# The last four blocks' gate and up in the 7-product form, and w_down of six blocks by token halves

## The chip, the cores and the metric

The kernel runs on one core of one Trainium2 chip, as one program. The metric is the device time of one execution in microseconds; lower is better. The engines that matter here are TensorE (PE in the profile; its weight loads are PEld), VectorE (DVE), ScalarE (ACT) and SyncE (SP), whose queue issues the kernel's transfers.

## The reference

One decoder layer on x of 1024 tokens by 1024 features, all in float32:

```python
x = _layer_norm(ALPHA * x + 0.5 * _swiglu(x, ffn1_w_gate[i], ffn1_w_up[i], ffn1_w_down[i]), ...)
mix = _token_mixer(x, w_in[i], ...)          # four GDN heads, four GLA heads, w_out
x = _layer_norm(ALPHA * x + mix, ...)
x = _layer_norm(ALPHA * x + 0.5 * _swiglu(x, ffn2_w_gate[i], ffn2_w_up[i], ffn2_w_down[i]), ...)

def _swiglu(x, w_gate, w_up, w_down):
    return (jax.nn.silu(x @ w_gate) * (x @ w_up)) @ w_down
```

The hidden width of each feed-forward layer (FFN) is 2816, that is 22 blocks of 128. The change is in the second FFN and the layer norm that ends the layer.

## The kernel before

**Numbers.** Every large product is made of three matmuls: each operand is split into a high part (a cast on ScalarE) and a low part (a subtraction on VectorE), and high by high, low by high and high by low are added up in one bank of PSUM. `split` (lines 139 to 141) is that pair of instructions, so the profile shows nearly all splits as L140 and L141. A weight half, a hidden half or an x tile is 128 partitions by 512 columns, 256 KB. It is loaded by SP into a staging tile (tag `wr`, seven of them) and split into tiles that TensorE reads.

**Tiles.** x stands transposed, by token half (512 tokens) and feature block: `xh[half][k]`, `xl[half][k]`, k from 0 to 7. The layer's output rows are eight tiles `acc[c]` of 128 tokens by 1024, four to a token half; w_down adds to them by columns 0 to 511 and 512 to 1023.

**Plain form.** `hidden` (line 358) makes one block of 128 hidden features: per token half 8 x 3 matmuls for gate and as many for up (`proj`, lines 212 to 215), each 512 columns wide. `down` (line 218) adds w_down of several blocks to one output half tile: 3 matmuls a block in a bank tagged `pd` (three of these), then one VectorE instruction (line 239) that scales the bank and adds it to `acc`.

**7-product form.** `ffn_pairs` (line 729) takes the blocks two at a time. Gate, and then up, of two blocks for both token halves is a 2 by 2 by 2 product of quarters; `project` (line 512) makes it from 7 products of 4 x 3 matmuls (lines 554 to 556) where the plain form has 8. For this `token_sums` and `last_sums` keep sums of x quarters (named P5, P6, P3 and P7; P7 is written over x tiles 10 to 13, half 1, k 0 to 3), and `weight_sums` (line 479) makes sums of weight quarters on VectorE. `PRODUCTS` (line 47) is the order: P1, P2, P6, P5, P7, P4, P3. P1 and P2 read x of the first token half, P4 reads x tiles 14 to 17. The four results are complete after P2 (first half, first block), P7 (second half, second block), P4 (second half, first block) and P3 (first half, second block). The function given as `hidden` takes each result; `put` (line 568) writes it to device memory some turns later.

**Down steps.** w_down of the pairs' blocks is interleaved with the products. Two groups of four blocks use a 7-product form as well (`down_four`, lines 688 to 693, 28 steps of 6 matmuls each). Blocks 16 and 17 are done plainly (`down_two`, 16 steps of 6 matmuls through `down`). `STEPS` (line 53) says how many steps go with each pair; within a pair they are spread over its 14 products. Operands are made up to five (`DEEP`) ahead of their use.

**Order of the second FFN.** Blocks 0 to 7 are done plainly, partly beside the mixer. Then `ffn_pairs(2, range(8, 18))` does blocks 8 to 17 in five pairs (line 1288). Then `last_blocks` (line 402) does blocks 18 to 21 plainly: it loads x tiles 10 to 13 again (`restore`), and for each token half makes four hidden blocks (gate and up weights are loaded and split anew for each half) and calls `last_downs` (line 412), which loads the four blocks' w_down (again for each half) and goes through the four token tiles: the column halves of one tile, its statistics (`out_stats`), and beside the next tile its rows (`out_rows`: normalise, scale, store). The last tile's second column half is cut in two of 256, so that the end is short.

**Who sets the order.** A framework puts the written program into one stream for each engine. It works from the written order, but an instruction whose inputs are there may be placed ahead of earlier written ones that still wait; semaphores follow from the tiles that are read and written. Each engine then goes through its stream in order, SP included.

## Time and profile before

| | |
|---|---|
| median of 3 runs | 2027.14 us (2026.97, 2027.14, 2030.98) |
| the profiled execution | 2030.06 us, of which the span from first to last instruction is 2028.3 us |
| granted TensorE clock, mean | 0.998 |
| moved by DMA | 313.63 MB, mean 155 GB/s |

The span is what the views of the profile cover, with time counted from its start; the other 1.8 us lie around it. The views used are the page (busy time of each engine, the chain of waits that ended last), the windows view (busy time in chosen stretches), the groups (instructions by line, tiles and shape, with count, busy time and the mean of one), the timeline (start, duration, engine, line, what is written and read, and in brackets idle time before it and what ended it), the waits and the DMA issues. A matmul's duration overlaps the next one's, so the spacing of starts is what it costs.

### The profile page before, as it was taken

What the parts mean: (1) busy time and instruction counts of PE and PEld (TensorE: products, weight loads), DVE (VectorE), ACT (ScalarE), POOL (GpSimd) and SP (SyncE); (2) the same over time, 40 slices, a digit from 0 to 9 for tenths busy, and PEclk for the clock granted to TensorE, in tenths of its full rate; (3) what the DMA queues carried; (4) which work ended last, traced back from release to release, by engine and by line L of the source; (5) the groups of instructions that cost most, each with busy time, mean ns of one, the idle gap of its engine ahead of it and who ended that gap; (6) DMA issues with size and microseconds to landing.
All of it is one profiled execution on the core that took longest, in us unless ns stands there. A gap on an engine that the chain in (4) does not pass through costs nothing.

```text
span 2028.3 us, 28810 instructions
## 1 busy us (share of the span) xinstructions
PE 1995.8 (98%) x9956; PEld 1632.1 (80%) x9956; DVE 1435.8 (71%) x3043; ACT 875.2 (43%) x1739; POOL 50.3 (2%) x87
## 2 busy tenths in 40 slices
PE   8999999999999999999999999999999999999998
PEld 7888888888888777788788777788788888888887
DVE  7677776545677787756887687657956657888565
ACT  5333433222554445445566545444433433334332
POOL 0000000000000000000000000000000000000000
PEclk9999999999999999999999999999999999999999
DMA  8755645655553444445364433333443336466431
GB/s 268 264 173 166 202 142 167 205 195 192 171 191 128 136 149 142 135 134 169 127 197 130 132 106 122 104 105 109 135 142 119 114 117 200 156 212 204 146 121 61
DMA packets 170930, 313.63 MB, mean 155 GB/s; under 512 B 19360, under 2 KB 19872, under 8 KB 170784
## 3 DMA queue, kind: packets, MB, share of 16 engines
q1 hardware_dynamic: 170784, 311.80, 48.1%
q8 instruction: 78, 1.28, 0.3%
q14 instruction: 68, 0.56, 0.1%
HBM read 244.61 MB, written 67.11 MB: 154 GB/s over the span
## 4 chain that ended last, share of the span: by engine, by line
PE 84%; DVE 8%; DMA 3%; ACT 3%; issue 2%; POOL 1%; SPq 0%; DVEq 0%; ACTq 0%; POOLq 0%
PE pa L212 11%; PE pa L213 11%; PE pa L215 11%; PE pa L554 6%; PE pa L555 6%; PE pa L556 6%; PE pd L234 5%; PE pd L236 5%; PE pd L235 5%; PE pm L689 1%; PE pm L688 1%; PE pm L690 1%; PE pm L1211 1%; DVE acc L239 1%; PE pm L810 1%
## 5 line engine op out<-in xcount | busy, mean ns | idle before, releaser
L140 ACT CAST wh<-wr 128x512 fp32r<-128x512 f32 (+1 forms) x485 | 298.3, 620 | 645.6 <-PE pa L213 201.6
L212 PE MATMUL pa<-xh,wh 128*128 128x512 f32 x1168 | 469.9, 402 | 9.3 <-ACT xh L140 5.6
L141 DVE TENSOR_TENSOR wl<-wr,wh 128x512 fp32r<-128x512 f32 (+1 forms) x485 | 329.5, 686 | 203.6 <-ACT wh L140 199.1
L213 PE MATMUL pa<-xl,wh 128*128 128x512 f32 x1168 | 461.4, 395 | 0.1
L215 PE MATMUL pa<-xh,wl 128*128 128x512 f32 x1152 | 454.1, 394 | 0.0
L212 PEld LDWEIGHTS pa<-xh,wh 128*128 128x128 f32 x1168 | 220.9, 189 | 56.0 <-ACT xh L140 6.3
L213 PEld LDWEIGHTS pa<-xl,wh 128*128 128x128 f32 x1168 | 220.9, 189 | 42.6 <-DVE xl L141 2.1
L215 PEld LDWEIGHTS pa<-xh,wl 128*128 128x128 f32 x1152 | 217.2, 189 | 43.2
L239 DVE SCALAR_TENSOR_TENSOR acc<-pd,acc 128x512 f32<-128x512 f32 x305 | 205.3, 685 | 50.5 <-PE pd L236 48.9
L234 PE MATMUL pd<-wh,hh 128*128 128x512 f32 x352 | 141.1, 405 | 1.5 <-ACT xf L283 1.5
L235 PE MATMUL pd<-wl,hh 128*128 128x512 f32 x352 | 139.5, 397 | 1.0 <-DVE wl L141 1.0
L236 PE MATMUL pd<-wh,hl 128*128 128x512 f32 x352 | 138.9, 397 | 0.0
L554 PE MATMUL pa<-xh,wh 128*128 128x512 f32 x320 | 125.5, 392 | 0.5 <-DVE gs L530 0.5
L555 PE MATMUL pa<-xl,wh 128*128 128x512 f32 x320 | 124.6, 389 | 0.0
L556 PE MATMUL pa<-xh,wl 128*128 128x512 f32 x320 | 124.6, 389 | 0.0
L154 ACT CAST wh<-wr 128x512 fp32r<-128x512 f32 x132 | 80.0, 620 | 84.4 <-PE pa L213 63.6
L155 ACT CAST wl<-wr 128x512 fp32r<-128x512 f32 x132 | 81.0, 618 | 42.8 <-PE pd L235 39.1
L234 PEld LDWEIGHTS pd<-wh,hh 128*128 128x128 f32 x352 | 66.3, 188 | 19.6 <-ACT hh L140 4.1
L236 PEld LDWEIGHTS pd<-wh,hl 128*128 128x128 f32 x352 | 66.1, 188 | 14.9 <-DVE hl L141 2.5
L234 PE MATMUL pd<-wh,gh 128*128 128x512 f32 (+1 forms) x194 | 75.8, 393 | 1.4 <-DVE acc L239 1.2
L235 PEld LDWEIGHTS pd<-wl,hh 128*128 128x128 f32 x352 | 66.4, 189 | 12.6 <-DVE wl L141 1.4
L236 PE MATMUL pd<-wh,gl 128*128 128x512 f32 (+1 forms) x194 | 75.1, 388 | 0.0
(399 smaller groups left out, 3478.5 us busy)
## 6 DMA issues: line engine op xcount, KB each, us to landing
wr<-gu SPq DMA_DIRECT2D x263, 256.0 KB, 3.1
wr<-wd SPq DMA_DIRECT2D x172, 256.0 KB, 2.9
kept<-wl SPq DMA_DIRECT2D x132, 256.0 KB, 2.2
wr<-kept SPq DMA_DIRECT2D x132, 256.0 KB, 2.8
wr<-win SPq DMA_DIRECT2D x116, 256.0 KB, 3.1
wr<-hid SPq DMA_DIRECT2D x106, 256.0 KB, 2.9
hid<-gs SPq DMA_DIRECT2D x44, 256.0 KB, 2.6
hid<-wr SPq DMA_DIRECT2D x32, 256.0 KB, 3.3
```

The source lines that it names most:

```text
L140: self.nc.scalar.copy(hi, src)
L141: self.nc.vector.tensor_tensor(lo, src, hi.bitcast(F32), ALU.subtract)
L212: nc.tensor.matmul(ps[:], hi[:, sl], xh[k][:], start=(k == 0), stop=False)
L213: nc.tensor.matmul(ps[:], hi[:, sl], xl[k][:], start=False, stop=(lo is None and k == KB - 1))
L215: nc.tensor.matmul(ps[:], lo[:, sl], xh[k][:], start=False, stop=(k == KB - 1))
L234: nc.tensor.matmul(p, hh[:, sl], wh[:, ds], start=(i == 0), stop=False)
L235: nc.tensor.matmul(p, hh[:, sl], wl[:, ds], start=False, stop=False)
L236: nc.tensor.matmul(p, hl[:, sl], wh[:, ds], start=False, stop=(i == n - 1))
L239: nc.vector.scalar_tensor_tensor(acc, p, scale / ALPHA, acc, ALU.mult, ALU.add, accum_out=None if sums is None else sums[:, d:d + 1])
L554: nc.tensor.matmul(ps[:], op[0][:, sl], xh[:], start=new, stop=False, skip_group_check=True)
L555: nc.tensor.matmul(ps[:], op[0][:, sl], xl[:], start=False, stop=False, skip_group_check=True)
L556: nc.tensor.matmul(ps[:], op[1][:, sl], xh[:], start=False, stop=q == 3, skip_group_check=True)
```

## The change

The last four blocks also go through `ffn_pairs`, now over blocks 8 to 21 in seven pairs. The queue of down steps then holds the two groups of four only, 56 steps, spread over pairs three to seven. Nothing of w_down of blocks 16 to 21 is in the steps; `last_blocks` does it, for six blocks, plainly, by token halves.

For the last pair `last_pair` takes the results: those of the first token half are split at once into x tiles that are no longer read (06 and 07); those of the second go to device memory. `last_blocks` has no gate and up and no `restore`. It loads and splits w_down once for both token halves, and the hidden halves of the first token half that are in memory, into x tiles that have come free (`x_room`) and into tiles of its own pool; later the second token half's hidden halves. The first group of the first token half is two token tiles side by side, in which block 21 comes last in both (`ahead` is 2). Staging tiles go from seven to ten.

```diff
-BUFS = {"w": 6, "h": 3, "xf": 3, "wr": 7, ...
+BUFS = {"w": 6, "h": 3, "xf": 3, "wr": 10, ...
-STEPS = {1: (0, 14, 14, 18, 18), 2: (0, 0, 14, 14, 20)}
+STEPS = {1: (0, 14, 14, 18, 18), 2: (0, 0, 10, 10, 12, 12, 12)}
-LAST = 4
+LAST = 6
 def down(...):
-                                               accum_out=None if sums is None else sums[:, d:d + 1])
+                                               accum_out=sums[c][:, d:d + 1] if sums and c in sums else None)
 def out_stats(...):
-            self.rows = [self.ln_row(2, 0), self.ln_row(2, 1, ("hh", "hl"), BUFS["h"])]
+            self.rows = [self.ln_row(2, 0), self.ln_row(2, 1, ("g1", "b1"))]
+    def x_room(self, n):
+        return [self.wt(self.xp, [HT], f"x{e}{n // KB}{n % KB}", 1, F32R) for e in "hl"]
+
+    def last_pair(self, f):
+        def take(n, t=None):
+            if t is None:
+                return
+            if n[0] == "1":
+                hl = self.first_half[f + int(n[1]) - 1] = self.x_room(5 + int(n[1]))
+                self.split(hl[0][:], hl[1][:], t[:])
+            else:
+                self.put((f, 1, int(n[1]) - 1), t)
+        return take
+
     def last_blocks(self, fs):
         with self.phase("ep") as fx:
             self.hp = fx
-            self.scr = "xf", fx
-            for k in range(KB // 2):
-                self.restore(1, k)
-            for half in range(2):
-                hs = [now(self.hidden(2, f, (half,), fx, ("gh", "gl"), BUFS["g"])) for f in fs]
-                self.last_downs(fs, hs, half, fx)
+            free = list(range(6)) + list(range(8, 16))
+            def parts(t):
+                hl = self.x_room(free.pop(0)) if free else [self.wt(fx, [HT], "g" + e, len(fs) + 4, F32R) for e in "hl"]
+                self.split(hl[0][:], hl[1][:], t[:])
+                return hl
+            ws = [[parts(self.load(self.a["wd2"][f][:, HALVES[0]]))] for f in fs]
+            hs = [parts(self.load(self.hbm[(2, f - f % 2), 0, f % 2][:])) for f in fs[:-2]] + [self.first_half[f] for f in fs[-2:]]
+            for w, f in zip(ws, fs):
+                w.append(parts(self.load(self.a["wd2"][f][:, HALVES[1]])))
+            self.last_downs(hs, ws, 0, ([0, 1], [2], [3]))
+            hs = [parts(self.load(self.hbm[(f - f % 2, 1, f % 2) if f in fs[-2:] else ((2, f - f % 2), 1, f % 2)][:])) for f in fs]
+            self.last_downs(hs, ws, 1, ([0], [1], [2], [3]))
-    def last_downs(self, fs, hs, half, fx):
-        ws = [self.weight(self.a["wd2"][f], *((fx, "f") if 2 * n < BUFS["f"] else ())) for n, f in enumerate(fs)]
-        for c in range(4):
+    def last_downs(self, hs, ws, half, groups):
+        before = range(4)[-1:] if half else []
+        for cs in groups:
...
+            work = self.down(hs, ws, half, 0.5, cs, sums,
+                             ((0, HT), (HT, HT + HT // 2), (HT + HT // 2, D)) if last else ((0, HT), (HT, D)), len(cs))
...
 def ffn_pairs(...):
-        queue = [(idx, f, 4) for f in fours] + [(idx, f, 2) for f in range(start + 8, fs.stop, 2)]
+        queue = [(idx, f, 4) for f in fours] + [(idx, f, 2) for f in range(start + 8, fs.stop, 2) if idx == 1]
-            take = self.lone_pair(g) if g[1] not in fours else ...
+            take = self.last_pair(f) if f == NF - 2 else self.lone_pair(g) if g[1] not in fours else ...
 def run(self):
-            self.ffn_pairs(2, range(K2, NF - LAST), 0, beside=...)
+            self.ffn_pairs(2, range(K2, NF), 0, beside=...)
+            for _ in range(2):
+                self.turn += 2
+                self.put_now()
         self.last_blocks(range(NF - LAST, NF))
```

## The prediction

> **What bounds the kernel now.** I read the page first, for the engines' totals and the chain of waits.

> ```profile
> span 2028.3 us, 28810 instructions
> PE 1995.8 (98%) x9956; PEld 1632.1 (80%) x9956; DVE 1435.8 (71%) x3043; ACT 875.2 (43%) x1739; POOL 50.3 (2%) x87
> PE 84%; DVE 8%; DMA 3%; ACT 3%; issue 2%; POOL 1%; SPq 0%; DVEq 0%; ACTq 0%; POOLq 0%
> ```

> TensorE is busy 98% of the span and makes 84% of the chain. An average hides stages, so the second view is the windows view, cut where the timeline of TensorE changes from one kind of matmul to the next. The columns are window, length, then busy time (instructions) of PE, PEld, DVE, ACT and POOL, granted clock, DMA share and GB/s.

> ```profile
> 600.00:1460.00 860.00, 844.05 (x4842) 685.88 (x4841) 643.79 (x1738) 429.54 (x963) 40.37 (x61) 1.00 0.42 133
> 1598.72:1852.66 253.94, 253.94 (x1117) 208.92 (x1115) 184.85 (x294) 97.29 (x171) 0.00 (x0) 1.00 0.52 167
> 1852.66:1866.26 13.60, 13.60 (x62) 11.27 (x60) 12.54 (x22) 5.39 (x9) 0.00 (x0) 1.00 0.72 233
> 1866.26:1889.53 23.27, 22.36 (x97) 17.86 (x96) 18.07 (x30) 7.44 (x13) 0.00 (x0) 1.00 0.57 169
> 1889.53:1933.05 43.52, 43.52 (x193) 36.04 (x192) 18.84 (x28) 16.34 (x28) 0.00 (x0) 1.00 0.46 141
> 1933.05:1954.82 21.77, 21.77 (x97) 18.01 (x96) 16.63 (x38) 7.32 (x17) 1.66 (x3) 1.00 0.18 70
> 1954.82:1998.34 43.52, 43.52 (x193) 36.04 (x192) 23.29 (x39) 15.73 (x27) 0.84 (x1) 1.00 0.35 113
> 1998.34:2028.30 29.96, 22.11 (x109) 18.52 (x107) 20.99 (x48) 5.19 (x13) 2.55 (x4) 0.91 0.19 73
> ```

> In order these are: the mixer; the five block pairs in the 7-product form with the first down steps between; the rest of the second group of four; w_down of blocks 16 and 17; gate and up of the last four blocks for the first token half; their w_down; the same two for the second half, with the tail. From 1598.72 on TensorE is never idle except in the 1866.26 window and the tail, and in the stage that the change replaces VectorE and ScalarE are far from full. There the time is the number of matmuls times the spacing of two. The timeline's first column (start) gives that spacing:

> ```profile
> 1880.01 0.39 PE L234 MATMUL pd<-wh,gh 128*128 128x512 f32 x1
> 1880.24 0.39 PE L235 MATMUL pd<-wl,gh 128*128 128x512 f32 x1
> ```

> It is 0.23 us (the 0.39 is the length of one, overlapping the next); closer, 43.52 us over the 192 matmuls that the code issues there is 0.2267 us. [...]

> **Gate and up of blocks 18 to 21.** The grouped view of the last stages (line, operands, count) shows what goes:

> ```profile
> L212 PE MATMUL pa<-xh,wh 128*128 128x512 f32 x128 | 49.8, 389 | 0.0
> L213 PE MATMUL pa<-xl,wh 128*128 128x512 f32 x128 | 49.8, 389 | 0.0
> L215 PE MATMUL pa<-xh,wl 128*128 128x512 f32 x128 | 49.8, 389 | 0.0
> ```

> That is 3 x 128 = 384 matmuls. In their place come two more pairs: 2 pairs x 2 (gate, up) x 7 products x 4 chunks x 3 = 336. The difference is 48 x 0.2267 = 10.9 us off TensorE, the one engine that is full here. [...]

> **w_down.** The two groups of four keep their 336 matmuls. Blocks 16 and 17 (96) and 18 to 21 (96, then 84 of 512 and 24 of 256 columns, since the last token tile is cut) become six blocks in one form: 144, then 126 and 36. So 6 fewer of 512 and 12 more of 256 columns, whose spacing is read here, with the tail:

> ```profile
> 2020.05 0.28 PE L235 MATMUL pd<-wl,gh 128*128 128x256 f32 x1
> 2020.17 0.28 PE L236 MATMUL pd<-wh,gl 128*128 128x256 f32 x1
> 2020.95 0.41 DVE L239 SCALAR_TENSOR_TENSOR acc<-pd,acc 128x256 f32<-128x256 f32 x1
> 2024.51 0.99 SPq L334 DMA_DIRECT2D out_dram<-acc  x2
> ```

> 12 x 0.12 - 6 x 0.2267 = +0.1 us: nothing.

> **The stall that goes.** The 1866.26 window is 23.27 us for 96 matmuls, 21.77 us at the spacing, so it loses 1.5 us. Most of it is one place:

> ```profile
> 1874.57 0.39 PE L236 MATMUL pd<-wh,gl 128*128 128x512 f32 x1
> 1875.78 0.50 PE L234 MATMUL pd<-wh,gh 128*128 128x512 f32 x1 [0.82 <-DVE acc L239]
> ```

> Two-block sums hold a bank for only 6 matmuls (1.36 us), and VectorE, late with x splits and hidden splits, frees the banks late. Afterwards a sum takes 18 matmuls (4.1 us) with 0.60 us of VectorE to free it (starts below). I take -1.5 us. What is late next is the seam, below.

> **The tail.** The last matmul ends at 2020.17 + 0.28 = 2020.45, its accumulation starts at 2020.95: VectorE was still with the rows of the tile before. A token tile then has 8.2 us of matmuls rather than 5.4, so those rows are done sooner: -0.5 us. The rest is the same code.

> **More 7-product work.** The 1598.72 window holds 840 + 276 = 1116 matmuls, 253.0 us, and takes 253.94: 0.9 us lost over ten gate or up halves. Four more cost +0.4 us.

> **The seam.** The new wait is at the start of w_down for the first token half. It needs six split w_down halves, four hidden halves loaded back (blocks 16 to 19), and both blocks of the last pair, one of which leaves the last product. The x tiles that receive them come free after the last up half's second product (x00 to x05) and its P7 (x10 to x13). After that second product TensorE still has five products of 2.72 us and six steps of 1.36 us: 21.8 us of cover. What must fit in it is priced by these rows, the first two the pace of VectorE, the next three the landing (last column, us):

> ```profile
> 1861.40 0.68 DVE L693 SCALAR_TENSOR_TENSOR acc<-pd,acc 128x512 f32<-128x512 f32 x1
> 1862.00 0.68 DVE L141 TENSOR_TENSOR gl<-wr,gh 128x512 fp32r<-128x512 f32 x1
> wr<-wd SPq DMA_DIRECT2D x172, 256.0 KB, 2.9
> wr<-hid SPq DMA_DIRECT2D x106, 256.0 KB, 2.9
> hid<-gs SPq DMA_DIRECT2D x44, 256.0 KB, 2.6
> ```

> Ten loads are 2.6 MB, 11 us at the 233 GB/s of the 1852.66 window, and ten staging tiles let all be under way at once. Ten lower parts on VectorE are 6.0 us; its own work there is some 73% of 21.8, 16 us, less about 4 us because weight parts are made five operands ahead and run out before the end: 18 of 21.8. It fits, narrowly. The block from the last product (add, multiply, cast, subtract: 2.7 us) is hidden by the step behind that product, 1.36 us, and by the order of the first group, whose two tiles take that block last, 30 matmuls or 6.8 us in. The six halves for columns 512 to 1023 are due 36 matmuls, 8.2 us, after the start and cost 3.6 us of VectorE. I take +0.5 us for the whole seam, with 0 below (it cannot give time) and 7.7 above (first rival).

> What joins SP's queue: 10, then 6, then 6 loads and the four writes of the last pair's hidden halves, which wait for VectorE; only loads due later stand behind them. The second half's tokens go through memory (write 2.6 us, load 2.9) and are due 144 matmuls, 32.6 us, later. Dropped are the four x restores and 16 of 32 gate and up weight loads. All this lies beside TensorE: zero, unless VectorE fills.

> **The sum.** -10.9 + 0.1 - 1.5 - 0.5 + 0.4 + 0.5 = -11.9 us. The profiled execution spans 2028.3 us and took 2030.06; it would span 2016.4 and take 2018.2. The median of the runs, 2027.14, lies 2.9 below the profiled one; less 11.9 that is **2015.2 us**.

> **Rival 1: the seam opens.** The splits are written behind the last product. If ScalarE and VectorE keep that order, nothing starts before the last product ends: 2.7 us for its block, then seven splits at 0.60 and a first cast, 4.8 us, less the step's 1.36: 6.1 us idle. A pause also slows what follows:

> ```profile
> 1003.69 0.40 PE L236 MATMUL pd<-wh,hl 128*128 128x512 f32 x1
> 1005.88 0.80 PE L212 MATMUL pa<-xh,wh 128*128 128x512 f32 x1 [1.79 <-DVE wh L824]
> 1006.47 0.63 PE L213 MATMUL pa<-xl,wh 128*128 128x512 f32 x1
> ...
> 1008.61 0.63 PE L212 MATMUL pa<-xh,wh 128*128 128x512 f32 x1
> 1009.03 0.49 PE L234 MATMUL pd<-wh,hh 128*128 128x512 f32 x1
> ```

> After 1.8 us idle seven matmuls take from 1005.88 to 1009.03, 3.15 us, a spacing of up to 0.43 us where 7 x 0.2267 is 1.59: 1.6 us more. That makes 7.7 in all, and the time 2015.2 - 0.5 + 7.7 = 2022.4. [...] Against this rival: work written later does run earlier where its inputs are there.

> ```profile
> 1870.97 0.62 ACT L140 CAST xh<-wr 128x512 fp32r<-128x512 f32 x1 [0.92 <-DMA wr<-x2d]
> 1873.79 1.14 ACT L140 CAST gh<-wr 128x512 fp32r<-128x512 f32 x2
> ```

> The x casts of the last blocks stand ahead of hidden casts of blocks 16 and 17, which the code writes first. Chance 0.14.

> **Rival 2: slower, by the mixer.** Ten staging tiles serve the whole kernel, and a different arrival of weights gives ScalarE and VectorE another order between 600 and 1460 us, where TensorE waits on short chains.

> ```profile
> PEld pm L1083 <- ACT mi L1081: 9.5, 28, 0.4
> ```

> There 860 - 844.05 = 16 us are idle. A weight split that runs ahead of a chain's step delays it by 0.60 us. Slower by 0.2% (4.1 us, about what a measurement of this kernel can tell from no change) needs 11.9 + 4.1 = 16 us, or 27 such delays, as much idle time again: 2031.3 or more. Against it: the six pairs of split-weight tiles stay, and they, not the staging, decide when a split may run. Chance 0.07. The same shuffle could also give back a quarter of those 16 us.

> **Rival 3: the second column half is late.** If none of its six splits is done when the first group ends, 3.6 us more: 2018.8. For it: VectorE's narrow margin. Against: 8.2 us are due to it. Chance 0.07.

> **How the numbers follow.** The forecast has 0.72. Faster by over 0.2% (below 2023.0) are it, rival 3, and about a third of rival 1 after allowing for its coarse price: 0.84. Within 0.2%: the rest of rival 1, 0.08. Slower: rival 2, rounded up to 0.08 for what I have not thought of. The range reaches down to 2010 (no seam, and the quarter of 16 us gained) and up to 2023 (rival 1); it leaves out rival 2 and the ends of the others.

> **What would show it.** Right: no L212 to L215 group in the last 180 us; 1176 matmuls of L554 to L556's kind in the second FFN, not 840; from the first pair to the end of the last matmul some 410 us (before: 1598.72 to 2020.45, 421.7); TensorE unbroken between the last product and w_down; the mixer's idle time near 16 us. Wrong: a gap of microseconds at the seam with 0.43 us spacing behind it (rival 1), over 25 us idle in the mixer (rival 2), or gaps within the first token half that VectorE's splits end (rival 3).

## The result, and the profile after

| | before | after |
|---|---|---|
| median of 4 runs | 2027.88 us (2026.97 to 2030.98) | 2014.47 us (2013.18 to 2017.16) |
| ratio, 95% interval | | 0.9933 [0.9916, 0.9950] |
| profiled execution | 2030.06, span 2028.3 | 2013.18, span 2011.4 |

Faster by 13.4 us, where 11.9 were forecast; 2014.47 lies 0.7 below the predicted 2015.2, and the other 0.7 is in the kernel before, whose median is 2027.88 with a fourth run. Below, "the pairs' stretch" is the time from the first block pair of the second FFN to the end of the last matmul. It is the part of the kernel that the change rewrites.

The page of after, span, busy time and chain of waits:

```profile
span 2011.4 us, 28705 instructions
PE 1982.5 (99%) x9914; PEld 1622.3 (81%) x9914; DVE 1429.9 (71%) x3037; ACT 869.3 (43%) x1733; POOL 50.3 (3%) x87
PE 86%; DVE 8%; ACT 2%; DMA 2%; issue 1%; POOL 0%; SPq 0%; DVEq 0%; ACTq 0%; POOLq 0%
```

TensorE has 42 matmuls fewer (48 gone, 6 gained by finer cuts) and is still what bounds the kernel. The windows view of after, with the same columns as before (window, length, then busy time and instructions of PE, PEld, DVE, ACT, POOL, clock, DMA share, GB/s), shows the mixer, the pairs, the stretch just ahead of w_down, w_down of the first and of the second token half, and the tail:

```profile
600.00:1460.00 860.00, 844.82 (x4850) 686.50 (x4849) 646.77 (x1742) 430.13 (x964) 40.31 (x61) 1.00 0.42 134
1594.76:1938.83 344.07, 344.02 (x1513) 283.10 (x1511) 244.57 (x388) 135.43 (x237) 0.00 (x0) 1.00 0.47 154
1900.00:1938.83 38.83, 38.83 (x173) 31.96 (x171) 31.43 (x51) 19.17 (x33) 0.00 (x0) 1.00 0.56 173
1938.83:1971.50 32.67, 32.67 (x146) 27.07 (x145) 21.71 (x47) 9.36 (x21) 1.65 (x3) 1.00 0.26 93
1971.50:2004.50 33.00, 33.00 (x163) 27.89 (x161) 20.49 (x47) 4.57 (x12) 2.54 (x4) 1.00 0.16 65
2004.50:2011.40 6.90, 0.00 (x0) 0.00 (x0) 3.92 (x8) 0.00 (x0) 0.90 (x1) 0.88 0.20 76
```

TensorE has no gap worth naming from the first pair to the last matmul. VectorE is at 81% (31.43 of 38.83) ahead of w_down: close, not full. The mixer has 860 - 844.82 = 15.2 us idle, before 15.95: no reordering to speak of.

The pairs' stretch in one row, first before, then after:

```profile
1598.72:2020.45 421.73, 420.81 (x1860) 346.65 (x1858) 290.57 (x485) 154.70 (x276) 4.14 (x7) 1.00 0.47 150
```

```profile
1594.76:2004.50 409.74, 409.69 (x1818) 338.06 (x1816) 286.78 (x481) 149.36 (x270) 4.19 (x7) 1.00 0.43 142
```

So the 16.9 us by which the two spans differ are 12.0 in this stretch, 0.95 in the tail (7.85 to 6.90) and 4.0 ahead of the first pair, where the change edits nothing but the number of staging tiles. The last part is taken up with the experiments: some 2 us of it go with the number of staging tiles, and 1.6 are a short time at half the TensorE clock in the profile of before (clock column 0.50 from 1005.83 to 1009.24).

The seam, in the timeline of after (start, duration, engine, line, operands, in brackets idle time before it and what ended it). The last step of the pairs ends in L719, w_down begins in L235:

```profile
1938.60 0.39 PE L719 MATMUL pm<-wh,gl 128*128 128x512 f32 x1
1938.83 0.39 PE L235 MATMUL pd<-xh,xh 128*128 128x512 f32 x1
...
1931.76 2.67 ACT L141 CAST xh<-wr 128x512 fp32r<-128x512 f32 x4 [1.76 <-PE pa L585]
1939.11 0.63 ACT L141 CAST xh<-gs 128x512 fp32r<-128x512 f32 x1 [4.68 <-DVE gs L569]
...
1935.60 0.68 DVE L142 TENSOR_TENSOR xl<-wr,xh 128x512 fp32r<-128x512 f32 x1
```

The spacing stays 0.23 us across the seam. The splits of w_down and of the hidden halves into x tiles (`xh<-wr`, `xl<-wr`) are over at 1936.3, although the code writes them behind the last product; they are 14, the ten needed at the start and four of the six for the second column half. Of what the first sums need, only the block of the last product (`xh<-gs`) is split behind the seam, and ScalarE waited 4.7 us for it without harm. The last two w_down halves and the second token half's hidden halves follow it.

The tail, in the timeline of after:

```profile
2004.22 0.28 PE L237 MATMUL pd<-gh,gl 128*128 128x256 f32 x1
2004.54 0.42 DVE L240 SCALAR_TENSOR_TENSOR acc<-pd,acc 128x256 f32<-128x256 f32 x1 [1.07 <-PE pd L237]
2007.92 0.99 SPq L335 DMA_DIRECT2D out_dram<-acc  x2
```

VectorE now waits for the last matmul and follows it by 0.04 us; before it came 0.50 behind. That is half of the 0.95; the rest lies behind it, in the last rows and their store.

### The profile page after: what moved, and what is told of

It is laid out like the page before. It is cut to its first block, busy times and chain, and to the rows that moved or that the text cites. A ratio compares the mean times of both kernels' runs of the same rounds, so it can differ in the third digit from the quotient of the medians.

```text
span 2011.4 us, 28705 instructions
## 1 busy us (share of the span) xinstructions
PE 1982.5 (99%) x9914; PEld 1622.3 (81%) x9914; DVE 1429.9 (71%) x3037; ACT 869.3 (43%) x1733; POOL 50.3 (3%) x87
## 4 chain that ended last, share of the span: by engine, by line
PE 86%; DVE 8%; ACT 2%; DMA 2%; issue 1%; POOL 0%; SPq 0%; DVEq 0%; ACTq 0%; POOLq 0%
PE pa L213 9%; PE pa L214 9%; PE pa L216 9%; PE pa L583 8%; PE pa L584 7%; PE pa L585 7%; PE pd L235 6%; PE pd L237 6%; PE pd L236 6%; PE pm L718 1%; PE pm L717 1%; PE pm L719 1%; PE pm L1240 1%; DVE wl L142 1%; PE pm L839 1%
## 5 line engine op out<-in xcount | busy, mean ns | idle before, releaser
L141 ACT CAST wh<-wr 128x512 fp32r<-128x512 f32 (+1 forms) x469 | 289.5, 620 | 666.7 <-PE pa L584 204.4
L142 DVE TENSOR_TENSOR wl<-wr,wh 128x512 fp32r<-128x512 f32 (+1 forms) x469 | 318.1, 685 | 195.1 <-ACT wh L141 185.8
L213 PE MATMUL pa<-xh,wh 128*128 128x512 f32 x1040 | 419.2, 403 | 9.2 <-ACT xh L141 5.3
L214 PE MATMUL pa<-xl,wh 128*128 128x512 f32 x1040 | 411.3, 396 | 0.1
L216 PE MATMUL pa<-xh,wl 128*128 128x512 f32 x1024 | 404.3, 395 | 0.0
L213 PEld LDWEIGHTS pa<-xh,wh 128*128 128x128 f32 x1040 | 196.3, 189 | 51.2 <-ACT xh L141 6.5
L240 DVE SCALAR_TENSOR_TENSOR acc<-pd,acc 128x512 f32<-128x512 f32 x289 | 194.2, 684 | 56.7 <-PE pd L237 55.0
L214 PEld LDWEIGHTS pa<-xl,wh 128*128 128x128 f32 x1040 | 196.4, 189 | 37.6 <-DVE xl L142 2.1
L216 PEld LDWEIGHTS pa<-xh,wl 128*128 128x128 f32 x1024 | 193.2, 189 | 38.2
L583 PE MATMUL pa<-xh,wh 128*128 128x512 f32 x384 | 150.6, 392 | 0.2 <-DVE sn L568 0.2
L584 PE MATMUL pa<-xl,wh 128*128 128x512 f32 x384 | 149.5, 389 | 0.0
L585 PE MATMUL pa<-xh,wl 128*128 128x512 f32 x384 | 149.5, 389 | 0.0
L235 PE MATMUL pd<-wh,hh 128*128 128x512 f32 x352 | 140.9, 404 | 1.5 <-ACT xf L284 1.4
L236 PE MATMUL pd<-wl,hh 128*128 128x512 f32 x352 | 139.4, 397 | 1.0 <-DVE wl L142 1.0
L583 PEld LDWEIGHTS pa<-xh,wh 128*128 128x128 f32 x384 | 72.1, 188 | 18.7 <-DVE sn L568 2.2
L585 PEld LDWEIGHTS pa<-xh,wl 128*128 128x128 f32 x384 | 72.1, 188 | 15.1
L584 PEld LDWEIGHTS pa<-xl,wh 128*128 128x128 f32 x384 | 72.1, 188 | 14.6
L235 PEld LDWEIGHTS pd<-wh,hh 128*128 128x128 f32 x352 | 66.2, 188 | 19.6 <-ACT hh L141 4.2
## 6 DMA issues: line engine op xcount, KB each, us to landing
wr<-gu SPq DMA_DIRECT2D x247, 256.0 KB, 3.4
wr<-wd SPq DMA_DIRECT2D x164, 256.0 KB, 3.0
kept<-wl SPq DMA_DIRECT2D x132, 256.0 KB, 2.1
wr<-kept SPq DMA_DIRECT2D x132, 256.0 KB, 3.0
wr<-win SPq DMA_DIRECT2D x116, 256.0 KB, 3.2
wr<-hid SPq DMA_DIRECT2D x110, 256.0 KB, 3.3
hid<-gs SPq DMA_DIRECT2D x50, 256.0 KB, 2.1
hid<-wr SPq DMA_DIRECT2D x32, 256.0 KB, 3.0
```

The lines of the kernel that those rows point to most:

```text
L141: self.nc.scalar.copy(hi, src)
L142: self.nc.vector.tensor_tensor(lo, src, hi.bitcast(F32), ALU.subtract)
L213: nc.tensor.matmul(ps[:], hi[:, sl], xh[k][:], start=(k == 0), stop=False)
L214: nc.tensor.matmul(ps[:], hi[:, sl], xl[k][:], start=False, stop=(lo is None and k == KB - 1))
L216: nc.tensor.matmul(ps[:], lo[:, sl], xh[k][:], start=False, stop=(k == KB - 1))
L235: nc.tensor.matmul(p, hh[:, sl], wh[:, ds], start=(i == 0), stop=False)
```

## The experiments

Each ratio is to the kernel before, run on the same chip in the same series. It is given with its 95% interval, and differs from the quotient of the two medians by up to 0.001. "Changed kernel" is the kernel of the change.

**Ten staging tiles alone.** The kernel before, with one size changed.

```diff
-BUFS = {"w": 6, "h": 3, "xf": 3, "wr": 7, ...
+BUFS = {"w": 6, "h": 3, "xf": 3, "wr": 10, ...
```

> The kernel before with ten staging tiles instead of seven, nothing else. Two theories. Count theory: the gain is the 48 matmuls, the stall and the tail; in the stages before the pairs of the second FFN staging depth changes nothing that counts, and the 4.0 us by which the changed profile reaches the first of these pairs earlier (1594.76 against 1598.72) are the spread between executions. Then this run is the kernel before within 0.1%, a ratio of 1.000, and its mixer (600 to 1460 us) keeps some 16 us idle. Staging theory: deeper staging itself gives about 4 us ahead of the pairs. Then the ratio is 0.998 and the first pair starts 4 us earlier.

Measured: 2027.62 against 2029.74, 0.9989 [0.9980, 0.9998]. The row of the pairs' stretch:

```profile
1595.33:2017.21 421.88, 420.85 (x1860) 346.59 (x1858) 288.80 (x485) 153.82 (x276) 4.13 (x7) 1.00 0.45 148
```

421.9 us, as before. Ten tiles alone give the stretch nothing; what small gain they give (0.4 to 4 us by the interval) lies outside it. The profiles show where. All kernels but the last of this section have a pause of 2.2 us on TensorE near 1000 us, ahead of the same matmul. It ends at 1003.2 to 1004.3 in the seven profiles with ten tiles, at 1005.9 to 1006.3 in the three with seven, and at 1009.0 in the one with eight. So ten tiles gain some 2 us before that point, by these profiles, and the measured ratio lies between the two theories.

Inside the stretch the tiles only move a loss. The stage of the two-block steps, in which the prediction found its stall, takes 22.15 us here rather than 23.27:

```profile
1864.12:1886.27 22.15, 22.15 (x98) 17.87 (x96) 17.44 (x28) 7.18 (x13) 0.00 (x0) 1.00 0.57 178
```

Instead TensorE waits for VectorE in pair three, where 1.17 us lie between two starts at 1692.55.

**The changed kernel with seven staging tiles.** The same edit the other way round, `"wr": 10` to `"wr": 7` in the changed kernel.

> The changed kernel with the seven staging tiles of before. Count theory: ahead of the pairs no difference; at the seam the last three of the ten loads wait for a split, which 21.8 us of cover hide, so 2014.5 us, ratio to the kernel before 0.993 to 0.994, no gap ahead of w_down. Staging theory: 4 us more than the changed kernel, 2018.5 us, ratio 0.9955. If the ten tiles are what keeps the seam closed: a gap of 2 to 4 us between the last product and w_down, with 0.43 us spacing behind it.

Measured: 2029.24, ratio 0.9988 [0.9977, 0.9998]. Nearly the whole gain is gone, and all expectations missed the place: the seam is unbroken here too (the 6.58 us that TensorE is idle in the stretch are the 2.97 and 3.61 of two stops elsewhere). TensorE stops at the first down step of pair three, and again at that of pair five. The timeline of the first stop, PE and then SP:

```profile
1682.23 0.39 PE L585 MATMUL pa<-xh,wl 128*128 128x512 f32 x1
1685.59 0.97 PE L717 MATMUL pd<-wh,gh 128*128 128x512 f32 x3 [2.97 <-ACT wh L141]
1687.35 0.63 PE L717 MATMUL pd<-wh,gh 128*128 128x512 f32 x1
1687.78 0.63 PE L718 MATMUL pd<-wl,gh 128*128 128x512 f32 x1
...
1676.97 0.45 SPq L601 DMA_DIRECT2D hid<-wr  x1
...
1680.36 0.32 SPq L601 DMA_DIRECT2D hid<-wr  x1
1680.77 1.25 SPq L485 DMA_DIRECT2D wr<-wd  x2
```

The step waits for a cast of w_down (`wh`, L141), the cast for its load, and SP issues the step's two loads from 1680.77 on, 1.7 us before it is due (1682.46). Just ahead of them in the queue are the last two of four writes `hid<-wr`: the sums of hidden halves that `second_pair` keeps in staging tiles until they are written to memory, and that wait for VectorE. In the changed kernel the same two loads go out from 1654.19 on, 23 us before their step (1677.11) and ahead of all four writes. So with fewer tiles the framework places these loads later in SP's stream:

```profile
1654.19 2.65 SPq L485 DMA_DIRECT2D wr<-wd  x2
...
1668.90 1.04 SPq L601 DMA_DIRECT2D hid<-wr  x2
```

The second stop is longer:

```profile
1790.62 0.39 PE L585 MATMUL pa<-xh,wl 128*128 128x512 f32 x1
1794.62 0.97 PE L717 MATMUL pd<-wh,gh 128*128 128x512 f32 x3 [3.61 <-ACT wh L141]
```

Less a normal spacing each, the two stops are (3.36 - 0.23) + (4.00 - 0.23) = 6.9 us; behind the first, matmuls go at 0.43 us from 1686.92 to 1689.91, and behind the second the one at 1795.88 lasts 0.52 us, where the one before it took 0.39. Pair five, like pair three, follows a pair that makes such sums. The pairs' stretch is 420.4 us for the same 1818 matmuls, 10.7 more than with ten tiles.

**Eight staging tiles**, `"wr": 10` to `"wr": 8`.

> The changed kernel with eight staging tiles, steps as in the change. Theory of held tiles: with eight held at the first step of pairs three and five, eight tiles still leave none for the w_down loads, so stops of 2 to 4 us remain there, somewhat shorter than in E2, ratio 0.996 to 0.998. If one tile is enough to let the first load through: stops under 1 us, ratio 0.9935 to 0.995.

Measured: 2026.09, ratio 0.9974 [0.9964, 0.9984], in the range that the theory of held tiles gave. Its second stop in the timeline:

```profile
1789.56 0.40 PE L719 MATMUL pd<-wh,gl 128*128 128x512 f32 x1
1792.24 1.09 PE L717 MATMUL pd<-wh,gh 128*128 128x512 f32 x2 [2.29 <-ACT wh L141]
```

From start to start that is 2.7 us here and 1.4 at 1684.75, in the same two pairs, shorter than with seven (the one at 1684.75 below the 2 to 4 us expected), and the stretch takes 415.8. SP's queue ahead of the first stop lies between the other two: one of the two loads goes out behind two of the four writes, the other behind all four.

```profile
1675.39 1.05 SPq L601 DMA_DIRECT2D hid<-wr  x2
...
1678.11 0.43 SPq L485 DMA_DIRECT2D wr<-wd  x1
1678.63 0.88 SPq L601 DMA_DIRECT2D hid<-wr  x2
...
1681.71 0.33 SPq L485 DMA_DIRECT2D wr<-wd  x1
```

The cost falls with every tile added: 420.4, 415.8, 409.7 us with seven, eight and ten.

**Seven tiles, and the steps of before's first pairs.** In the kernel before, seven tiles cause no such stop. There the pairs three and four take 14 steps each, here 10, so that the first step comes later in the pair and its operands, made five ahead, are asked for among later weights.

```diff
-BUFS = {... "wr": 10, ...     STEPS = {..., 2: (0, 0, 10, 10, 12, 12, 12)}
+BUFS = {... "wr": 7, ...      STEPS = {..., 2: (0, 0, 14, 14, 10, 10, 8)}
```

> The changed kernel with seven staging tiles and the steps at 14, 14, 10, 10, 8 instead of 10, 10, 12, 12, 12. Run E2 stopped TensorE for 3.4 and 4.0 us at the first down step of pairs three and five, not at the seam. Theory of held tiles: with 10 steps the first step stands behind the pair's second product, so four raw gate or up tiles are loaded ahead of its w_down and stay in use, beside four that the pair before still holds for its sums: eight, one more than there are. With 14 steps it stands behind the first product, two raw tiles ahead, six in all, and the w_down loads find room: no stop over 1.5 us there, ratio 0.9935 to 0.995, the rest of the way to E2 being what ten tiles give ahead of the pairs. If seven tiles are too few for seven pairs whatever the order: stops as in E2 and a ratio of 0.998 or more.

Measured: 2024.13 (2019.43 to 2025.84), ratio 0.9968 [0.9956, 0.9980], between the expectations. The profile has no stop at 1682: the two loads go out at 1656.59 and 1665.55, ahead of the four writes (from 1672.45 on). It has 1.7 us at 1781.9 (a wait for VectorE) and 1.0 us at 1797.6 (again for a cast of w_down), around the start of pair five, which has 10 steps here; its stretch is 412.4 us. So the step schedule explains the first stop; the later ones are shorter with it, and not gone. The profiled execution was this kernel's shortest; what the others lose beyond it was not seen.

**Gate and up alone.** The changed kernel, with w_down of blocks 16 and 17 in the steps and of 18 to 21 by token halves, as before.

```diff
-STEPS = {..., 2: (0, 0, 10, 10, 12, 12, 12)}    LAST = 6
+STEPS = {..., 2: (0, 0, 14, 14, 14, 14, 16)}    LAST = 4
-        queue = ... for f in range(start + 8, fs.stop, 2) if idx == 1]
+        queue = ... for f in range(start + 8, fs.stop if idx == 1 else NF - LAST, 2)]
```

> One part of the change alone: gate and up of the last four blocks in the 7-product form, but w_down of blocks 16 and 17 stays in the down steps (72 steps: 14, 14, 14, 14, 16 with pairs three to seven), and four blocks are left for the end by token halves. Count theory: the 48 matmuls are all gone here too, so 10.9 us less, and up to 1.5 us more if the two-block steps no longer stall now that products lie between them: 2015.5 to 2017 us, ratio 0.994 to 0.995. If instead w_down of six blocks alone carries the gain: less than half of it here, 2021 us or more.

Measured: 2017.76 against 2029.74, ratio 0.9931 [0.9919, 0.9944]: as fast as the changed kernel (0.9933 and 0.9917 in two other series), as far as the timing tells. The row of the stretch, and then VectorE near the end:

```profile
1596.81:2007.68 410.87, 409.78 (x1812) 337.60 (x1810) 294.88 (x496) 150.56 (x272) 4.19 (x7) 1.00 0.42 142
```

```profile
2006.80 0.75 DVE L333 SCALAR_TENSOR_TENSOR acc<-xf,mv,b 128x512 f32<-128x512 f32 x1
...
2008.45 0.41 DVE L240 SCALAR_TENSOR_TENSOR acc<-pd,acc 128x256 f32<-128x256 f32 x1
```

In the profiles it stands 1.1 us behind the changed kernel in the stretch and 1.1 in the tail (2007.68 to the end of the span at 2015.7 is 8.0). The tail shows why: VectorE is still with the rows of the tile before (L333) when the last sums come, and starts the last one 0.8 us behind the last matmul. The 1.1 of the stretch is one stop: TensorE waits for VectorE from 1694.12 to 1695.54 in pair three, as the kernel before does with ten tiles. So the rest of the change, w_down of six blocks and the steps that this leaves, is worth some 2 us by two profiles; the timings don't resolve it.

**48 matmuls put back.** The changed kernel makes P1 of the last two pairs twice, over the same bank: 2 pairs x 2 (gate, up) x 12 matmuls more.

```diff
-            for q, (xh, xl) in enumerate(self.tokens(n)):
+            for q, (xh, xl) in list(enumerate(self.tokens(n))) * (2 if twice and n == "P1" else 1):
-                make = self.project(ops, hid, up, take)
+                make = self.project(ops, hid, up, take, idx == 2 and f >= NF - 4)
```

> The changed kernel with 48 matmuls put back: in the last two pairs the first product of each gate and up half is made twice (the second time overwrites the first with the same values), on operands that are there anyway; nothing else is added. Count theory (TensorE is full in the pairs, so 48 matmuls are 48 x 0.2267 us): 10.9 us more than the changed kernel, ratio to the kernel before 0.9987. If the gain came from the other engines' relief or from staging, the repeat would lie beside them: under half of that, ratio 0.996 or less.

**The changed kernel once more**, in the same series, as its yardstick.

> The changed kernel once more, on the chip and in the rounds of the other three, with its own profile. Ratio 0.9933 as measured before, within 0.001. The stretch from the first pair of the second FFN to the last matmul repeats to 0.5 us (409.7 us); what differs between its executions lies ahead of it, where a pause near 1003 us is or is not followed by half-rate matmuls (1.5 us).

Measured: 2024.81, ratio 0.9972 [0.9961, 0.9983], and 2013.37, ratio 0.9917 [0.9904, 0.9930]. The rows of the stretch, with the 48 and without:

```profile
1596.78:2017.32 420.54, 420.54 (x1866) 347.07 (x1864) 287.23 (x481) 149.27 (x270) 4.20 (x7) 1.00 0.42 139
```

```profile
1598.14:2007.78 409.64, 409.64 (x1818) 337.99 (x1816) 286.73 (x481) 149.37 (x270) 4.19 (x7) 1.00 0.43 142
```

48 matmuls, 10.90 us in the stretch and 11.4 in the medians: the main term of the sum, by itself. (The expectation counted its ratio from 0.9933; against the yardstick of its own series it is 0.0055, that is 11.2 us.) The second row also shows how well a stretch repeats: 409.64 here, 409.74 in the first profile of the same program, while the first pair starts at 1598.14 and 1594.76. Of the 3.4 us between these two, the last section shows the cause: in the second profile TensorE has half its clock for 6.8 us near 1003, in the first never there. Of the 4.0 us between before and after, 2.1 are there when the pause near 1000 ends (1005.88 and 1003.80), and 1.6 come right behind it, from half the clock for 3.41 us in before: 19 matmuls behind the end of the pause the two are 6.04 and 4.46 us on (1011.92 and 1008.26).

**The splits in their written order.** The changed kernel, with the casts and subtractions of `last_blocks` held where the code writes them.

```diff
-    def split(self, hi, lo, src):
-        self.nc.scalar.copy(hi, src)
-        self.nc.vector.tensor_tensor(lo, src, hi.bitcast(F32), ALU.subtract)
+    def split(self, hi, lo, src, pin=lambda i: i):
+        pin(self.nc.scalar.copy(hi, src))
+        pin(self.nc.vector.tensor_tensor(lo, src, hi.bitcast(F32), ALU.subtract))
...
-                self.split(hl[0][:], hl[1][:], t[:])
+                self.split(hl[0][:], hl[1][:], t[:], self.tc.keep_in_program_order)
```

> The changed kernel with every split that the last stage writes pinned on ScalarE and VectorE behind all that is written before it, so that the w_down and hidden splits wait for the last product of the last pair (rival 1 of the prediction, made to happen). By the prediction's working: 6.1 us idle between the last product and w_down and 1.6 us of half-rate matmuls behind it, 7.7 us in all, about 2022 us, ratio 0.997. If the seam is covered whichever way the splits stand: 2014.5 us and no gap.

Measured: 2022.91, ratio 0.9961 [0.9948, 0.9975]. The first rival, made to happen; PE and then ScalarE in the timeline:

```profile
1937.99 0.39 PE L719 MATMUL pm<-wh,gl 128*128 128x512 f32 x1
1942.81 0.50 PE L235 MATMUL pd<-xh,xh 128*128 128x512 f32 x1 [4.43 <-ACT xh L141]
...
1944.11 0.79 PE L237 MATMUL pd<-xh,xl 128*128 128x512 f32 x1 [0.56 <-DVE xl L142]
...
1950.24 0.40 PE L236 MATMUL pd<-xl,xh 128*128 128x512 f32 x1
...
1938.50 0.62 ACT L141 CAST xh<-gs 128x512 fp32r<-128x512 f32 x1 [13.10 <-DVE gs L569]
1939.03 6.34 ACT L141 CAST xh<-wr 128x512 fp32r<-128x512 f32 x12
```

ScalarE stands for 13.1 us in front of the last product's cast, and does twelve casts in a row when TensorE needs them. The pause is 4.82 - 0.23 = 4.6 us, a second wait adds 0.8 by 1944.11, and from there 13 matmuls take 1950.24 - 1944.11 = 6.13 us, where 13 x 0.2267 is 2.95: 3.2 more. That makes 8.6 us at the seam. Another 1.3 us are lost at 1980.6, where the second half's hidden splits were held as well, a place that the rival had not priced. The stretch is 419.64 us, 9.9 longer.

**Token tiles one by one.** The changed kernel, with `([0], [1], [2], [3])` for `([0, 1], [2], [3])` in the first `last_downs`, so that the block of the last product is due 15 matmuls after the seam rather than 30.

> The changed kernel, but the first token half goes through w_down one token tile at a time, not with its first two side by side. The prediction counted the pairing as cover for the block from the last product (2.7 us of add, multiply, cast and subtract; due 1.36 + 6.8 us later). Unpaired, that block is due after the last step and five other blocks of one sum, 1.36 + 3.4 = 4.8 us, still later than 2.7, and the second column half after 18 matmuls instead of 36, when its splits are already done in the changed profile. By that: the same time within 0.5 us, ratio 0.9917 to 0.9933, no gap over 0.3 us behind the last product. If the pairing is what keeps the seam closed: a gap of 1 to 3 us in the first two sums and up to 5 us in all with half-rate matmuls, ratio 0.9945 or so.

Measured: 2015.39, ratio 0.9935 [0.9921, 0.9948], stretch 409.85 us, no gap at the seam. The pairing of two tiles isn't needed as cover: the splits are early anyway.

**An earlier load in the mixer.** All eleven other profiles have a pause of 2.2 us on TensorE near 1002 to 1009, ahead of the second token half's small mixer inputs. (The expectation's count is off: there were ten such profiles by then, and half rate followed in five of them; it did in six of the eleven.) Here those inputs are started one layer norm sooner.

```diff
+                early = self.misc(1)
+                next(early)
                 self.ln(0, 1)
...
-            tasks = [self.misc(half), prep(ORDER[0], half)]
+            tasks = [early if half else self.misc(half), prep(ORDER[0], half)]
```

> The changed kernel with the split of the mixer's first weight block for the second token half written ahead of the layer norm instead of behind it. In all eight other profiles of this study TensorE pauses 2.0 us at 1002 to 1005 us for that split, and in five of them half-rate matmuls follow for 1.4 to 2.9 us. If this pause is what makes executions of one program differ ahead of the pairs: the pause is gone, no half-rate matmuls in that place, and the time is 2 to 3.5 us below the changed kernel's, ratio 0.990 to 0.992, with less spread between executions. If the pause only moves to the next thing that is late (x, behind the same layer norm): no change, 0.9917 to 0.9933.

Measured: 2013.27, ratio 0.9922 [0.9908, 0.9935]. That pause is gone; five others of 0.6 to 1.0 us stand between 1003 and 1035, and half the clock comes behind the last of them, from 1037.16 to 1040.58. The changed kernel had 0.9933 and 0.9917, so no gain can be claimed. Its four runs spread by 1.1 us, where two series of four of the changed kernel spread by 4.0 and 4.8.

## Why the prediction was right, and where it was not

**The 48 matmuls: right.** -10.9 us forecast; putting them back costs 10.90 us in the stretch. Gate and up alone carries nearly all of the gain.

**The rest of the stretch.** Forecast -11.4, measured -12.0. At 0.2267 us for 512 and 0.12 for 256 columns, the 1860 matmuls of before take 1836 x 0.2267 + 24 x 0.12 = 419.1 us, so 2.6 were lost there; the 1818 of after take 1782 x 0.2267 + 36 x 0.12 = 408.3, so 1.4 are lost. Instead of -1.5 (the stall), +0.4 (more halves) and +0.5 (the seam), in all -0.6, the losses fell by 1.2. The rows tell the terms apart. The pairs of after take 344.07 us for 1512 matmuls, 1.3 over the spacing, where before lost 0.9: the +0.4 came as forecast. The 1.5 of the two-block steps are gone, as forecast; w_down of six blocks loses 0.1 (32.67 + 33.00 us, less 270 x 0.2267 and 36 x 0.12). The term that was off is the seam: 0 rather than +0.5. The size of the stall term is in part luck, though: with ten tiles alone that stage loses 0.4 and pair three the rest, so most of the loss didn't belong to the two-block sums as such.

**The seam: right in mechanism.** The splits run early and VectorE's margin came out close: 18 of 21.8 us forecast; in the last 21.8 us before the seam it is busy for 17.55.

```profile
1917.03:1938.83 21.80, 21.80 (x98) 17.86 (x96) 17.55 (x29) 10.11 (x17) 0.00 (x0) 1.00 0.64 199
```

That it is so close is in part luck. Three of the ten lower parts lie ahead of these 21.8 us, because x00 to x03 are read by the first product alone and come free a product earlier than the prediction has it (the first of their splits starts at 1913.03); and four of the second column half, which the 18 did not count, lie inside.

The third rival (second column half late) fell with it: four of its six halves were ready at the start. Of the two covers that the prediction named for the last product's block, the order of the first group proved unneeded.

**The first rival: did not occur, and was priced a little low.** 7.7 us forecast, 8.6 when made to happen: 4.6 of idle time rather than 6.1, but 3.2 rather than 1.6 at half rate, and a second wait of 0.8. The surcharge was taken from one pause where seven matmuls ran slowly; here thirteen did: the slow spacing lasted 6.13 us rather than 3.15.

**The tail: right in mechanism, mis-sized.** -0.95 rather than -0.5. The wait of the last sum for VectorE went from 0.50 to 0.04 us, and the kernel that has the old w_down with the new gate and up still has it.

**The step that failed: the staging tiles.** The prediction has ten tiles as something that helps the seam ("let all be under way at once"), and says of weights in general that the split-weight tiles, "not the staging, decide when a split may run". With seven tiles the seam is unbroken, and the gain is gone by another mechanism: ahead of the first down step of pairs three and five the w_down loads stand in SP's queue behind the writes of four sums that are kept in staging tiles, and TensorE stops for 3 to 4 us each time. The prediction priced the steps' new spacing (10, 10, 12, 12, 12 for 14, 14, 20) at nothing without asking which buffers are held when a first step falls due. It came out right because the change itself brought the tiles. Also, the "slower" rival had the wrong place: what would have taken the gain away lay in the pairs, not in the mixer. And the sum has no term for what ten tiles give ahead of the pairs, some 2 us. With it the parts add up to 12.0 + 0.95 + 2, about 15; the two series measured 13.4 and 17.2 between their medians, so the closeness of the first to 11.9 is in part luck.

Shown are the place, the wait (a cast of w_down that waits for its load, which is issued late), the load's place among the four writes with seven, eight and ten tiles, and that more tiles or an earlier first step shorten or move the stop. Which tile each load waited for was only argued: read from the code, four raw quarters of the next gate and the four sums of hidden halves, eight in all, would fit with stops at seven and eight and none at ten. Nine tiles weren't tried.

## What to carry to other kernels

Where TensorE runs unbroken, count matmuls and multiply by the spacing of their starts (0.2267 us here for 512 columns); the sum held within 0.1 us for 48 of them. When a schedule of interleaved steps changes, list for the first step of each stage which buffers are held at that moment and where its load stands in the queue: a gain of 13 us hung on three staging tiles whose need shows nowhere in the profile of before. Compare kernels by the stretch that was edited, which repeated within 0.1 us, rather than by the whole span, which moved by 3.3 us between two profiles of one program; and where an edit reaches beyond the stretch, as the staging tiles do, compare a fixed point ahead of it too.

## What the runs showed of the hardware that was not expected

The same pause is followed by full rate or by half rate. The timeline of the changed kernel near 1000 us in its first profile,

```profile
1001.62 0.40 PE L237 MATMUL pd<-wh,hl 128*128 128x512 f32 x1
1003.80 0.50 PE L213 MATMUL pa<-xh,wh 128*128 128x512 f32 x1 [1.79 <-DVE wh L853]
```

and in its second:

```profile
1001.94 0.40 PE L237 MATMUL pd<-wh,hl 128*128 128x512 f32 x1
1004.11 0.79 PE L213 MATMUL pa<-xh,wh 128*128 128x512 f32 x1 [1.77 <-DVE wh L853]
1004.70 0.63 PE L214 MATMUL pa<-xl,wh 128*128 128x512 f32 x1
...
1009.82 0.52 PE L235 MATMUL pd<-wh,hh 128*128 128x512 f32 x1
```

One program, one pause of 2.2 us from start to start; the second time the matmuls go at 0.43 us from 1004.11 to 1009.82, 13 of them in 5.71 us where 2.95 would do: 2.8 us lost. Of eleven profiles six show it, with six to twelve full matmuls of 0.63 us. This one place makes most of the 3.3 us between the two spans.

The clock column of the windows view, the share of the TensorE clock that was granted, shows when half rate begins and ends. First the second profile of the changed kernel, ahead of half rate and during it, then the profile of gate and up alone:

```profile
999.83:1003.24 3.41, 1.77 (x7) 0.80 (x6) 3.33 (x7) 3.41 (x7) 0.00 (x0) 1.00 0.24 82
1003.24:1010.07 6.83, 5.96 (x14) 4.69 (x15) 4.26 (x9) 2.23 (x5) 0.00 (x0) 0.50 0.57 192
```

```profile
1004.82:1008.23 3.41, 3.41 (x9) 2.65 (x9) 2.01 (x4) 0.16 (x1) 0.00 (x0) 0.50 0.85 299
```

Half the clock lasts 6.83 us in the first of these and 3.41 us in the second. The other spells are read from the starts: with seven tiles, with the 48 matmuls put back and with single token tiles they are 0.43 us apart for 3.3 to 3.4 us behind this pause (1007.58 to 1010.97, 1005.70 to 1008.97, 1006.09 to 1009.34), and behind the splits in written order for longer, from 1944.11 to 1950.24. Half rate need not begin with the pause: with gate and up alone the pause ends at 1003.61, and the matmuls still start 0.23 us apart until the clock falls at 1004.82.

The profile of before, ahead of half rate, during it, up to the next fall of the clock, and from there to the end of the span:

```profile
1002.42:1005.83 3.41, 0.97 (x3) 0.49 (x3) 3.32 (x7) 3.41 (x7) 0.00 (x0) 1.00 0.33 116
1005.83:1009.24 3.41, 3.36 (x8) 2.69 (x9) 2.74 (x5) 1.41 (x3) 0.00 (x0) 0.50 0.68 225
1009.24:2023.00 1013.76, 1002.03 (x5016) 820.94 (x5015) 723.27 (x1542) 440.59 (x878) 24.39 (x34) 1.00 0.43 137
2023.00:2028.25 5.25, 0.00 (x0) 0.00 (x0) 2.15 (x4) 0.00 (x0) 0.57 (x1) 0.50 0.27 100
```

What decides between full and half rate behind the pause stays open. In the 3.41 us ahead of half rate TensorE was busy for 0.97 us in before and for 1.77 in the second profile of the changed kernel. In its first the clock does not fall before the tail, at 2009.77; 295 times 3.4133 ahead of that is 1002.84, inside the pause, and in the 3.41 us on either side of it TensorE was busy for 1.86 and 2.45:

```profile
999.43:1002.84 3.41, 1.86 (x7) 0.90 (x6) 3.32 (x7) 3.41 (x7) 0.00 (x0) 1.00 0.22 78
1002.84:1006.25 3.41, 2.45 (x11) 2.03 (x12) 3.41 (x7) 2.32 (x5) 0.00 (x0) 1.00 0.67 201
```

But with ten tiles alone the pause lies within one such step, 1002.53 to 1005.95. By the starts TensorE was busy there for 1.6 us, from 1004.32 on, and the matmuls stay 0.23 us apart; with gate and up alone it was busy for as long ahead of half rate (1001.41 to 1004.82).

The busy time in the windows view does not show this loss: a matmul at half rate counts as busy throughout. In the row of the pairs' stretch with seven staging tiles TensorE is idle for 6.6 us,

```profile
1600.02:2020.45 420.43, 413.85 (x1818) 339.78 (x1816) 287.47 (x481) 149.78 (x270) 4.18 (x7) 0.99 0.44 140
```

yet the stretch is 10.7 us longer than with ten for the same 1818 matmuls: some 4 us went into wider spacing, and two spells of 3.41 us at half the clock would be 3.4 of them, an estimate. The starts in the timeline show the spells; the clock column, averaged to 0.99 here, barely does.
